# Hybrid encoder block on one core: steps that take another engine's result put off in a queue between matmuls

## The chip, the cores and the metric

The kernel runs on one core of a Trainium2 chip. Its engines work side by side, each through its own list of instructions in order: TensorE (PE, matmuls and transposes), VectorE (DVE), ScalarE (ACT), GpSimd (POOL), and SyncE (SP), which here only issues DMA transfers. An instruction starts when those ahead of it on its engine are through and what it reads or overwrites is free. The metric is the device time of one execution in microseconds (us); less is better.

## The reference

One block of a bidirectional encoder, in float32, on 1024 tokens of width 1024 (`D_MODEL`), with one input projection, gated linear attention with 4 heads, a pooling branch with 4 channel groups, a merge, and a feed-forward part (SwiGLU, inner width 2816):

```python
h = rmsnorm(x, norm_mix[l])
proj = h @ w_in[l]
q, k, v, r, lr_f, lr_b, u, g_a, g_b = jnp.split(proj, split_points, axis=-1)
...
o = o_fwd + o_bwd
o = o * lax.rsqrt(jnp.mean(o * o, axis=-1, keepdims=True) + EPS)
...
o = (o * jax.nn.silu(r.astype(jnp.float32))).astype(x.dtype)
y_a = o @ w_branch_gla[l]

pooled = multiscale_pool(u)
y_b = jnp.einsum('blgc,gcd->blgd', pooled, w_pool_group[l]).reshape(bsz, length, D_MODEL)
y_b = (y_b * pool_scale[l]).astype(x.dtype)

merged = jax.nn.sigmoid(g_a) * y_a + jax.nn.sigmoid(g_b) * y_b
x = x + merged @ w_out[l]

h2 = rmsnorm(x, norm_ffn[l])
gate, up = jnp.split(h2 @ w_ffn_in[l], 2, axis=-1)
x = x + (jax.nn.silu(gate) * up) @ w_ffn_out[l]
...
return rmsnorm(x, norm_final)
```

`o_fwd` and `o_bwd` are the scans of the attention in both directions, in chunks; `multiscale_pool` takes centred means over 2, 4, 8 and 16 tokens, less the token.

## The kernel before

**Products.** Each float32 operand is split in two: a high part, the cast to the matmul type (`wh`, `dh`, `oh`, `ph`: a cast on ACT, line 182), and a low part, the operand less its high part (`wl`, `dl`, `ol`, `pl`: a subtract on VectorE or POOL, line 183). A product is three matmuls, high by high, high by low and low by high, of 128x128 by 128x512 (line 256). The helper `split_to` writes the cast and, right behind it, the subtract. Large projections take seven products of half size in place of eight (Strassen's scheme as Winograd arranged it): sums of blocks are made ahead of products, sums of results behind them.

**Stages**, in order of time: the norm of `x`; the projections of queries, keys and values with the attention beside them (25 to about 345 us); the output gate and its transposes (to 393); ten gate runs of seven products, for pool input and merge gates (393 to 606), with the pooled sums beside them; the branch projection with `w_branch_gla` (606 to 690), whose results are merged with the gates; the projection with `w_out` (to 776); the units of the feed-forward part (to about 1200); its output projection (to 1415); the end.

**Order.** The program is written out by one Python function, and each engine executes in the order in which the function came to its instructions. Work for the other engines is spread between the matmuls by `pump(dt)`, called after each product of three, with 1 for 512 columns (three matmuls, 0.68 us) and 0.5 for 256. It moves three lists on: `pending` (weights to be split), `aside` (jobs that `beside` writes one step at a time, `every` so many units) and `side` (generators: the attention, `pooling` and `features`, each `yield` being the units until its next step).

**Names that the change touches.**
- `branch_piece` makes what a product of the branch projection needs: `load` issues the DMA of the weights (`wraw`), `sums` the block sums of the attention's output (`ob`, `t`, on VectorE), `make` the two casts and subtracts of the weights (`wh` on ACT, `wl` on POOL) and then `data_split`, the cast `dh` and subtract `dl`. `merged_piece` does the same in the `w_out` projection, from the merged blocks `mg` and their sums `s`, with the data first. `project` calls `line_make` one piece ahead.
- `merge` and `collect_branch` take the results of the branch off TensorE's banks: three operations per bank (lines 1326, 1328, 1329).
- `Gates.run` takes the results of a gate run off the banks: sums `ga` on VectorE (line 1194), a copy (1189) or sigmoid (1197) on ACT.
- `pooled` makes the pooled sums of a group (`ws`, VectorE) and splits them (`ph`, `pl`); `pooling` loads their input `u`, and stores the parts in `p_out`. `load_pool_weights` and `split_pool_weights` bring the group's small weights (`wpr`, split in `wph` and `wpl`), `load_pooled` the parts back.
- The raw weights of the gate runs are `fraw`, their block sums `fs`.
- `features` transposes the normed rows `xn` and splits them for the feed-forward units.
- `whole(t)` is the final norm and the store of a block of 128 rows: squares on ACT, `n3rs` on VectorE and POOL, the scaling `res` on VectorE, and the store on SP. It is called for four blocks, where the fifth of the seven products of the last projection ends. `split_piece` splits the next operands there (`wor`, `gor` to `oh`, `ol`).

Of the kernel before, what the change touches and what calls it, by code (L numbers as in the profile page):

```python
# [17 lines left out]
P = 128  # L18
# [25 lines left out]
PUT = 3  # L44
POOLING = 2.2

# [5 lines left out]
def kernel(  # L52
# [93 lines left out]
    pending, credit = [], [0.0]  # L146

    def pump(dt):
        if pending:
            credit[0] += dt  # L150
            if credit[0] >= 2:
                credit[0] = 0.0
                pending.pop(0)()
        if aside:
            aside[0][1] -= dt
            if aside[0][1] <= 0:
                cost = next(aside[0][0], None)
# [354 lines left out]
    def unit_jobs(n):  # L512
# [5 lines left out]
        for op, p, src in (  # L518
            (None, 1, a11), (None, 4, a22), (None, 2, a12), (partial(padd, a22, a21, a22), 5, a22),
            (partial(psub, a21, a11, a21), 7, a21), (partial(psub, a11, a22, a11), 6, a11),  # L520
            (partial(psub, a12, a12, a11), 3, a12),
        ):
            yield op, src, u_out[n][p]
# [32 lines left out]

    def beside(jobs, every, put):

        cast = differ = None
        puts = [[] for _ in range(put)]  # L560
        while True:
            job = next(jobs, None)
            if not any((job, cast, differ, *puts)):
                return
# [3 lines left out]
            if differ:  # L568
# [4 lines left out]
                else:  # L573
                    right.setdefault(dst, []).append((hi, lo))
            differ = None
            if cast:
# [3 lines left out]
                differ = src, parts, dst  # L580
            cast = None
            if job:
                op, src, dst = job
                if op:
                    op()
                if src is not None:
                    cast = src, dst
# [5 lines left out]
    def prepare_beside(jobs, every, put=PUT):  # L593
        aside.append([beside(chain(*jobs), every, put), every])

# [19 lines left out]
    def attention(h, q, k):  # L615
# [120 lines left out]
        kts = {(1, 1): transposed_keys(1, 1)}  # L736
        yield 5.0
        while h not in v_heads:
# [25 lines left out]
        p = scores(0)  # L764
        yield 4.5
        o = [slot(shape=(4, DV), s="o") for _ in range(2)]
# [209 lines left out]
    def pooled(g, u, hi, lo):  # L976
        width = WINDOWS[g]
        n = HALF + 2 * PAD
        for half in range(2):
# [18 lines left out]
            yield 1  # L998
            split_to(hi[:, half, :], lo[:, half, :], s[:, body])
            yield 1  # L1000


# [34 lines left out]
    def data_split(src):  # L1037
        hi, lo = slot(F32R, s="dh"), slot(F32R, s="dl")
        split_to(hi[:, :, :], lo[:, :, :], src[:, :, :])
        return [(hi[:, k, :], lo[:, k, :]) for k in range(2)]  # L1040
# [27 lines left out]
    def branch_piece(p, c):  # L1068
# [10 lines left out]
        def make(raw):  # L1079
            b = {1: ob[0, 0], 2: ob[1, 0], 3: ob[1, 1], 4: ob[1, 0], 5: ob[0, 0], 6: t2s, 7: ob[0, 1]}[p][c]  # L1080
            return weight_split(raw), data_split(b)

# [60 lines left out]
    def pooling():  # L1143

        for g in range(GROUPS):
# [7 lines left out]
            for cost in pooled(g, u, hi, lo):  # L1153
                yield POOLING * cost
            yield 2
            for n, t in enumerate((hi, lo)):
# [72 lines left out]
    for n, run in enumerate(gate_runs):  # L1229
# [4 lines left out]
        if n == 7:  # L1234
            finish_side()
            finish_beside()
            prepare_beside(map(unit_jobs, range(READY)), 3.2, 1)
        if last:
            finish_beside()
        for at, (of, p) in enumerate(run):  # L1240
# [7 lines left out]
            if at == 4:  # L1248
                flush()
                if n == 2:  # L1250
                    begin(pooling(), 4)
            if n >= 6:
                if at == 0:
                    load_pool_weights(n - 6)
                if at == (0 if last else 3):
                    load_pooled(n - 6)
                elif at == 4:
                    split_pool_weights(n - 6)
            if last and at == 1:
# [15 lines left out]
    def project(base, products, collect, before, amid=None, first=FIRST, up=UP, pools_of=lambda p: U_BANKS if p == 1 else X_BANKS):  # L1275
        banks = {}
        for at, p in enumerate(products):
# [4 lines left out]
            for c in range(2):  # L1282
                n = base + 2 * at + c
                while len(made) <= n:
                    line_make()
                line_load()
                line_make()
# [342 lines left out]

    begin(features(1), 10)
    zs = {n: Gated(units[n], True) for n in range(3)}
# [49 lines left out]
    def whole(t):  # L1682

        ms, res = vec(4, "n3ms"), slot(shape=(D,), s="res")
        for j in range(2):
            squares(t, ms, res, j)
        rs = two_scale(ms)
        for j in range(2):
            nc.vector.scalar_tensor_tensor(
                res[:, COLS[j]], x2[t][:, COLS[j]], rs[:, :], gain_final[:, COLS[j]], op0=ALU.mult, op1=ALU.mult  # L1690
            )
        nc.sync.dma_start(out[t * P : (t + 1) * P, :], res[:, :])

# [43 lines left out]
    for at, p in enumerate(OUT_ORDER):  # L1737
# [4 lines left out]
        for i in range(CLOSE if closing else n_of):  # L1742
# [6 lines left out]
            for m in range(4):  # L1749
# [9 lines left out]
        if closing:  # L1759
            for m in range(4):  # L1760
                for i in range(CLOSE, n_of):
# [31 lines left out]
```

## Time and profile before

| | |
|---|---|
| median of 3 runs | 1425.53 us (1422.4 to 1426.63) |
| profiled execution | 1426.57 us |
| span of the profile | 1424.9 us |
| TensorE busy | 1379.3 us, 97% |
| VectorE, ACT, POOL busy | 857.6, 623.0, 746.2 us |
| mean granted TensorE clock | 0.992 |
| DMA | 243.62 MB, 171 GB/s over the span |

The span goes from the first to the last record of the profile, and the 1.7 us between it and the execution's time lie around it. TensorE is the engine that is busy nearly all the time, so its waits, and the stretches in which its granted clock is below 1, are what the profile has to be searched for. Each row of the waits names an engine and what it waited for last; the timelines give the start of each instruction, its duration, and in brackets the engine's idle time ahead of it.

### The profile page before, as it was taken

The numbers are of one execution on the slowest core, as the hardware profiler recorded it, in microseconds if no ns is written. First come the engines' busy times: TensorE is split into PE (matmuls) and PEld (weight loads), VectorE is DVE, ScalarE is ACT, GpSimd is POOL, SyncE is SP. The second block draws the span as 40 slices with busy tenths as digits, with TensorE's granted clock in tenths as the row PEclk, the third lists the DMA queues.
The fourth block names the chain that finished last, engine by engine and source line by source line (L and its number), as shares of the span: only waits on it lengthen the run. The fifth ranks groups of instructions, "written<-read, shape, count | busy, mean of one in ns | idle before, by whom it ended". The sixth has DMA issues, their size and how long they took to land. (4 is left out here: it accounts for less than half of the span.)

```text
span 1424.9 us, 18551 instructions
## 1 busy us (share of the span) xinstructions
PE 1379.3 (97%) x6677; PEld 1157.4 (81%) x6677; DVE 857.6 (60%) x1073; ACT 623.0 (44%) x1115; POOL 746.2 (52%) x558
## 2 busy tenths in 40 slices
PE   7999999999999999899999999999999999999997
PEld 6889898978888788677877788888888888888876
DVE  6166757667645674677875775565655556343374
ACT  6364655553234344453346633333333334443253
POOL 3252715123298455464665176666666667564254
PEclk9999999999999999999999999999999999999999
DMA  6221422322277568896513565544444447975361
GB/s 189 75 60 45 139 69 98 126 94 70 75 238 236 177 217 278 333 386 202 194 60 142 177 228 170 169 150 148 143 149 151 144 158 257 389 258 190 133 266 59
DMA packets 167612, 243.62 MB, mean 171 GB/s; under 512 B 10936, under 2 KB 98016, under 8 KB 167520
## 3 DMA queue, kind: packets, MB, share of 16 engines
q1 hardware_dynamic: 167520, 242.45, 50.4%
q8 instruction: 52, 0.85, 0.3%
q14 instruction: 40, 0.33, 0.1%
HBM read 164.55 MB, written 77.86 MB: 170 GB/s over the span
## 5 line engine op out<-in xcount | busy, mean ns | idle before, releaser
L183 POOL TENSOR_TENSOR wl<-fs,wh 128x512 fp32r<-128x512 f32 x120 | 166.2, 1389 | 174.7 <-ACT wh L182 130.9
L256 PE MATMUL ps<-gh,wh 128*128 128x512 f32 x616 | 240.4, 390 | 0.0
L256 PE MATMUL ps<-gl,wh 128*128 128x512 f32 x616 | 239.8, 389 | 0.0
L256 PE MATMUL ps<-gh,wl 128*128 128x512 f32 x616 | 239.7, 389 | 0.0
L183 POOL TENSOR_TENSOR wl<-fraw,wh 128x512 fp32r<-128x512 f32 x90 | 129.4, 1438 | 57.3 <-ACT wh L182 57.2
L256 PE MATMUL ps<-hh,wh 128*128 128x512 f32 x376 | 149.9, 399 | 0.0
L256 PE MATMUL ps<-hh,wl 128*128 128x512 f32 x376 | 146.8, 390 | 0.0
L256 PE MATMUL ps<-hl,wh 128*128 128x512 f32 x376 | 146.5, 390 | 0.0
L183 POOL TENSOR_TENSOR wl<-raw,wh 128x512 fp32r<-128x512 f32 x47 | 67.3, 1444 | 145.6 <-ACT wh L182 120.8
L183 POOL TENSOR_TENSOR ol<-gor,oh 128x1024 fp32r<-128x1024 f32 (+1 forms) x42 | 103.5, 2472 | 74.0 <-ACT oh L182 67.2
L256 PEld LDWEIGHTS ps<-gl,wh 128*128 128x128 f32 x616 | 115.6, 188 | 24.2 <-DVE gl L1395 0.4
L256 PEld LDWEIGHTS ps<-gh,wl 128*128 128x128 f32 x616 | 115.6, 188 | 24.0
L256 PEld LDWEIGHTS ps<-gh,wh 128*128 128x128 f32 x616 | 115.7, 188 | 23.6
L256 PE MATMUL ps<-ol,oh 128*128 128x512 f32 x308 | 120.6, 392 | 3.0 <-DVE ol L183 3.0
L256 PE MATMUL ps<-oh,oh 128*128 128x512 f32 x308 | 120.6, 392 | 1.4 <-DVE x L1716 1.4
L256 PE MATMUL ps<-oh,ol 128*128 128x512 f32 x308 | 120.3, 391 | 0.0
L183 POOL TENSOR_TENSOR wl<-wraw,wh 128x512 fp32r<-128x512 f32 x56 | 86.7, 1574 | 54.6 <-ACT wh L182 46.3
L183 DVE TENSOR_TENSOR ol<-wor,oh 128x1024 fp32r<-128x1024 f32 (+1 forms) x42 | 72.3, 1742 | 48.0 <-ACT oh L182 40.6
L182 ACT CAST wh<-fs 128x512 fp32r<-128x512 f32 x120 | 73.7, 615 | 32.5 <-DVE fs L852 28.8
L256 PEld LDWEIGHTS ps<-hh,wl 128*128 128x128 f32 x376 | 70.6, 188 | 15.2
L256 PEld LDWEIGHTS ps<-hl,wh 128*128 128x128 f32 x376 | 70.7, 188 | 13.2
L256 PEld LDWEIGHTS ps<-hh,wh 128*128 128x128 f32 x376 | 70.7, 188 | 13.3
(249 smaller groups left out, 3188.5 us busy)
## 6 DMA issues: line engine op xcount, KB each, us to landing
fraw<-in_w_ffn_in_dram SPq DMA_DIRECT2D x44, 512.0 KB, 6.0
gor<-g_out SPq DMA_DIRECT2D x35, 512.0 KB, 6.2
raw<-in_w_in_dram SPq DMA_DIRECT2D x48, 256.0 KB, 3.0
g_out<-s SPq DMA_DIRECT2D x44, 256.0 KB, 2.3
fraw<-in_w_in_dram SPq DMA_DIRECT2D x20, 512.0 KB, 6.6
wor<-t_out SPq DMA_DIRECT2D x20, 512.0 KB
g_out<-g SPq DMA_DIRECT2D x33, 256.0 KB, 2.6
x<-in_x_dram SPq DMA_DIRECT2D x16, 512.0 KB, 5.7
```

The lines of the kernel that those rows point to most:

```text
L182: nc.scalar.copy(hi, src)
L183: eng.tensor_tensor(lo, src, as_f32(hi), op=ALU.subtract)
L256: nc.tensor.matmul(ps, a[i], b[j], start=first and n == 0, stop=last and n == 2, skip_group_check=onto)
```

## The change

A fourth list, `put_off`, holds steps for later: `soon(delay, *steps)` puts them in, `pump` writes those whose delay has run out, `settle` writes all. In it go the low parts `dl` of the data in the branch and `w_out` projections (2 units after the cast), the scale of `whole` (2 units after the squares) and the rest of `whole` with its store (1.5 after that). In `branch_piece` the data is cast ahead of the weights. The queue is settled ahead of each piece that `project` takes up, and at the closing products.

```diff
+    put_off = []
+
+    def soon(delay, *steps):
+        put_off.extend([delay, step] for step in steps)
+
+    def settle():
+        while put_off:
+            put_off.pop(0)[1]()
+
     def pump(dt):
+        for entry in put_off:
+            entry[0] -= dt
+        while put_off and put_off[0][0] <= 0:
+            put_off.pop(0)[1]()
         if pending:
...
     def data_split(src):
-        hi, lo = slot(F32R, s="dh"), slot(F32R, s="dl")
-        split_to(hi[:, :, :], lo[:, :, :], src[:, :, :])
+        hi, lo = (slot(F32R, s=s)[:, :, :] for s in ("dh", "dl"))
+        src = src[:, :, :]
+        nc.scalar.copy(hi, src)
+        soon(2, partial(nc.vector.tensor_tensor, lo, src, as_f32(hi), op=ALU.subtract))
         return [(hi[:, k, :], lo[:, k, :]) for k in range(2)]
...
-            return weight_split(raw), data_split(b)
+            right = data_split(b)
+            return weight_split(raw), right
...
                 n = base + 2 * at + c
+                settle()
                 while len(made) <= n:
                     line_make()
+                    settle()
...
             squares(t, ms, res, j)
-        rs = two_scale(ms)
-        for j in range(2):
...
+        def scale():
+            rs = two_scale(ms)
+            soon(1.5, partial(finish, rs))
+
+        def finish(rs):
+            for j in range(2):
...
+            nc.sync.dma_start(out[t * P : (t + 1) * P, :], res[:, :])
+
+        soon(2, scale)
```

The pooled sums are spread otherwise: their steps come every 1.75 units in place of 2.2, cast and subtract of the split are two steps, and the stores come 4 units after in place of 2. The group's weights are loaded and split earlier in the gate runs. `beside` can hold its casts back by `lag` steps, which the jobs at run 7 use (`lag` 2), and the order of the first two blocks that these jobs prepare is turned. In the attention two delays are longer, and the features begin later.

```diff
-POOLING = 2.2
+POOLING = 1.75
...
             yield 1
-            split_to(hi[:, half, :], lo[:, half, :], s[:, body])
+            nc.scalar.copy(hi[:, half, :], s[:, body])
             yield 1
+            nc.vector.tensor_tensor(lo[:, half, :], s[:, body], as_f32(hi[:, half, :]), op=ALU.subtract)
+            yield 0.2
...
-            yield 2
+            yield 4
             for n, t in enumerate((hi, lo)):
                 nc.sync.dma_start(p_out[g][n], as_f32(t[:, :, :]))
...
-            prepare_beside(map(unit_jobs, range(READY)), 3.2, 1)
+            prepare_beside(map(unit_jobs, range(READY)), 3.1, 1, 2)
...
-            if n >= 6:
-                if at == 0:
-                    load_pool_weights(n - 6)
-                if at == (0 if last else 3):
-                    load_pooled(n - 6)
-                elif at == 4:
-                    split_pool_weights(n - 6)
+            if 5 <= n < 9 and at == 5:
+                load_pool_weights(n - 5)
+            elif n >= 6 and at == 2:
+                split_pool_weights(n - 6)
+            if n >= 6 and at == (0 if last else 3):
+                load_pooled(n - 6)
...
-        yield 5.0
+        yield 5.6
...
-        yield 4.5
+        yield 5.2
...
-            begin(features(0), 10)
+            begin(features(0), 11.5)
...
-    begin(features(1), 10)
+    begin(features(1), 12)
```

**Where it moves instructions.** First, the branch projection on VectorE, from the third product's sums to the first operation of `merge` (the names end in buffer numbers; `t_...` is the sum `t`). Before:

```order
L183 TENSOR_TENSOR dl_6032<-ob_5805,dh_6031 128x1024
L1062 TENSOR_TENSOR ob_5796<-ob_5833,ob_5796 128x1024
L1064 TENSOR_TENSOR t_1184_6036<-ob_5837,ob_5796 128x1024
L183 TENSOR_TENSOR dl_6081<-t_1184_6036,dh_6080 128x1024
L1062 TENSOR_TENSOR ob_5797<-ob_5834,ob_5797 128x1024
L1064 TENSOR_TENSOR t_1196_6085<-ob_5838,ob_5797 128x1024
L183 TENSOR_TENSOR dl_6122<-t_1196_6085,dh_6121 128x1024
L1326 TENSOR_TENSOR ps_6066<-ps_6066,sum_5967 128x512
```

And now, at the same place:

```order
L1080 TENSOR_TENSOR ob_5796<-ob_5837,ob_5796 128x1024
L1082 TENSOR_TENSOR t_1184_6035<-ob_5841,ob_5796 128x1024
L162 TENSOR_TENSOR dl_6024<-ob_5805,dh_6023 128x1024
L1080 TENSOR_TENSOR ob_5797<-ob_5838,ob_5797 128x1024
L1082 TENSOR_TENSOR t_1196_6084<-ob_5842,ob_5797 128x1024
L162 TENSOR_TENSOR dl_6073<-t_1184_6035,dh_6072 128x1024
L162 TENSOR_TENSOR dl_6114<-t_1196_6084,dh_6113 128x1024
L1346 TENSOR_TENSOR ps_6066<-ps_6066,sum_5967 128x512
```

Each pair of sums stands ahead of the `dl` that it stood behind, and the two last `dl` are together right ahead of the merge.

On ACT, a little earlier, at the first two pieces of the branch, before:

```order
L182 CAST wh_5880<-wraw_5800 128x512
L182 CAST wh_5884<-wraw_5800 128x512
L182 CAST dh_5888<-ob_5796 128x1024
L1197 ACTIVATE ga_5794<-ga_5794 128x512
L1197 ACTIVATE ga_5767<-ga_5767 128x512
```

And now:

```order
L1056 CAST dh_5880<-ob_5796 128x1024
L196 CAST wh_5883<-wraw_5800 128x512
L196 CAST wh_5887<-wraw_5800 128x512
L1216 ACTIVATE ga_5794<-ga_5794 128x512
L1216 ACTIVATE ga_5769<-ga_5769 128x512
```

The data's cast changed places with the two of the weights.

Second, the four final norms on VectorE, from the first sum `x` of the product behind which they come to the next `ol`. Before:

```order
L1716 TENSOR_TENSOR x_2134_10852<-ps_11493,x_2134_10852 128x512
L1461 TENSOR_SCALAR n3rs_11897<-n3ms_11893 128x1
L1689 SCALAR_TENSOR_TENSOR res_11894<-x_2134_10852,n3rs_11897,gfin_10843 128x512 x2
L1716 TENSOR_TENSOR x_2141_10890<-ps_11494,x_2141_10890 128x512
L1461 TENSOR_SCALAR n3rs_11911<-n3ms_11907 128x1
L1689 SCALAR_TENSOR_TENSOR res_11908<-x_2141_10890,n3rs_11911,gfin_10843 128x512 x2
L183 TENSOR_TENSOR ol_11918<-wor_11850,oh_11917 128x1024
L1716 TENSOR_TENSOR x_2148_10928<-ps_11495,x_2148_10928 128x512
```

And now:

```order
L1743 TENSOR_TENSOR x_2134_10852<-ps_11493,x_2134_10852 128x512
L1743 TENSOR_TENSOR x_2141_10890<-ps_11494,x_2141_10890 128x512
L197 TENSOR_TENSOR ol_11906<-wor_11850,oh_11905 128x1024
L1481 TENSOR_SCALAR n3rs_11916<-n3ms_11893 128x1
L1743 TENSOR_TENSOR x_2148_10928<-ps_11495,x_2148_10928 128x512
L1481 TENSOR_SCALAR n3rs_11927<-n3ms_11901 128x1
L1743 TENSOR_TENSOR x_2155_10966<-ps_11496,x_2155_10966 128x512
L1714 SCALAR_TENSOR_TENSOR res_11894<-x_2134_10852,n3rs_11916,gfin_10843 128x512 x2
L1481 TENSOR_SCALAR n3rs_11945<-n3ms_11920 128x1
```

The scaling `res` of a block stands behind the sums of all four, and the first `ol` ahead of all four.

Third, the gate runs on SP, around the second and third store of pooled parts. Before:

```order
L1157 DMA p_out<-ph_4745 128x1024
L1157 DMA p_out<-pl_4746 128x1024
L844 DMA fraw_4855<-in_w_in_dram 128x8x128
L1149 DMA u_4864<-u_rows_4147 128x520
L1150 DMA u_4865<-u_rows_4147 128x520
L450 DMA sa_out<-ga_4635 256x1x512
L450 DMA sa_out<-ga_4659 256x1x512
L844 DMA fraw_5001<-in_w_in_dram 128x8x128
L844 DMA fraw_5024<-in_w_in_dram 128x8x128
L1157 DMA p_out<-ph_4890 128x1024
```

And now:

```order
L1176 DMA p_out<-ph_4745 128x1024
L1176 DMA p_out<-pl_4746 128x1024
L1168 DMA u_4854<-u_rows_4147 128x520
L1169 DMA u_4855<-u_rows_4147 128x520
L858 DMA fraw_4861<-in_w_in_dram 128x8x128
L464 DMA sa_out<-ga_4636 256x1x512
L464 DMA sa_out<-ga_4661 256x1x512
L858 DMA fraw_5003<-in_w_in_dram 128x8x128
L1176 DMA p_out<-ph_4879 128x1024
```

The weights' load `fraw` that stood between the stores and the loads of `u` stands behind the loads of `u`, and the next run's second one behind the stores as well.

More of the change, by code (lines that the diff above doesn't have):

```diff
@@ L518, in unit_jobs @@
         for op, p, src in (
-            (None, 1, a11), (None, 4, a22), (None, 2, a12), (partial(padd, a22, a21, a22), 5, a22),
+            (None, 4, a22), (None, 1, a11), (None, 2, a12), (partial(padd, a22, a21, a22), 5, a22),
             (partial(psub, a21, a11, a21), 7, a21), (partial(psub, a11, a22, a11), 6, a11),
@@ L555, in parts_for, with beside @@
         return [slot(F32R, s=s)[:, :, :] for s in ("trh", "trl")]
-    def beside(jobs, every, put):
-        cast = differ = None
+    def beside(jobs, every, put, lag):
+        casts, differ = [None] * lag, None
         puts = [[] for _ in range(put)]
@@ L562, in beside @@
             job = next(jobs, None)
-            if not any((job, cast, differ, *puts)):
+            if not any((job, *casts, differ, *puts)):
                 return
@@ L574, in beside @@
                     right.setdefault(dst, []).append((hi, lo))
-            differ = None
+            differ, cast = None, casts.pop(0)
             if cast:
@@ L580, in beside @@
                 differ = src, parts, dst
-            cast = None
+            casts.append(None)
             if job:
@@ L586, in beside @@
                 if src is not None:
-                    cast = src, dst
+                    casts[-1] = src, dst
                 elif dst is not None:
@@ L591, in beside, with prepare_beside @@
             yield every
-    def prepare_beside(jobs, every, put=PUT):
-        aside.append([beside(chain(*jobs), every, put), every])
+    def prepare_beside(jobs, every, put=PUT, lag=1):
+        aside.append([beside(chain(*jobs), every, put, lag), every])
     def finish_beside():
@@ L1686, in whole @@
             squares(t, ms, res, j)
-        rs = two_scale(ms)
-        for j in range(2):
[L1689 to L1692, printed above, removed]
+        def scale():
[3 more added lines that the diff above has]
+            for j in range(2):
+                nc.vector.scalar_tensor_tensor(
+                    res[:, COLS[j]], x2[t][:, COLS[j]], rs[:, :], gain_final[:, COLS[j]], op0=ALU.mult, op1=ALU.mult
+                )
+            nc.sync.dma_start(out[t * P : (t + 1) * P, :], res[:, :])
+        soon(2, scale)
     def second_half(t):
@@ L1759 @@
         if closing:
+            settle()
             for m in range(4):
```

## The prediction

> **What bounds the kernel now.** I read the page's first part, then the waits of TensorE, then windows of its time, and last the timelines of the engines behind each wait. The first fence has the row of the page on TensorE and the rows of the waits view that matter here (engine, line, what was waited for: us in total, times, longest).
>
> ```profile
> PE 1379.3 (97%) x6677; PEld 1157.4 (81%) x6677; DVE 857.6 (60%) x1073; ACT 623.0 (44%) x1115; POOL 746.2 (52%) x558
> PE ps L256 <- DVE ga L1194: 5.3, 2, 2.9
> PE ps L256 <- DVE dl L183: 4.3, 1, 4.3
> PE tr L1410 <- DVE xn L292: 3.7, 3, 2.2
> PE ps L256 <- POOL wl L183: 3.5, 7, 1.3
> PE ps L256 <- DVE ol L183: 3.0, 1, 3.0
> PE ps L256 <- ACT ga L1189: 1.4, 2, 1.0
> PE yb L256 <- ACT wph L182: 1.2, 1, 1.2
> ```
>
> TensorE is busy 1379.3 of the 1424.9 us of the span, so 45.6 us are all that waiting costs directly, some 10 of them the tail behind the last matmul. The change takes no matmul away: it can only win back waits and what hangs on them. The windows show that (start:end, length, TensorE busy, its matmuls, granted clock, DMA share, GB/s).
>
> ```profile
> 475.00:500.00 25.00, 21.81 (x89) 0.93 0.54 168
> 495.21:498.62 3.41, 3.41 (x10) 0.50 0.01 2
> 600.00:625.00 25.00, 22.82 (x100) 1.00 1.01 382
> 641.98:648.81 6.83, 5.05 (x12) 0.50 0.70 224
> ...
> 720.51:723.92 3.41, 3.41 (x9) 0.50 0.00 0
> 800.00:825.00 25.00, 25.00 (x111) 1.00 0.43 146
> 1372.43:1375.85 3.42, 3.42 (x10) 0.50 1.03 408
> ```
>
> At 800–825 nothing is waited for: 111 matmuls. In 475–500 there are 89, because a wait of 2.9 us is followed by 3.41 us in which the clock is 0.50. Such a stretch costs half of its busy time, 3.41/2 = **1.7 us**; the one at 642–649 costs 5.05/2 = **2.5 us**. Two more of 3.41 us lie behind the waits at 718 (for POOL) and 1368 (for VectorE). So a wait of about 3 us costs 4.6, if its clock stretch goes with it.
>
> [...]
>
> **Branch projection: the data cast ahead of the weights, the subtract put off.** Timelines: start, us, engine, line, operands, and in brackets idle time before it.
>
> ```profile
> 597.22 1.14 ACT L182 CAST wh<-wraw 128x512 fp32r<-128x512 f32 x2 [3.28 <-DMA wraw<-in_w_branch_gla_dram]
> 598.26 1.05 ACT L182 CAST dh<-ob 128x1024 fp32r<-128x1024 f32 x1
> ...
> 622.15 1.14 ACT L182 CAST wh<-wraw 128x512 fp32r<-128x512 f32 x2 [4.03 <-DMA wraw<-s_out]
> 623.20 1.05 ACT L182 CAST dh<-t 128x1024 fp32r<-128x1024 f32 x1
> ```
> ```profile
> 599.35 2.17 DVE L183 TENSOR_TENSOR dl<-ob,dh 128x1024 fp32r<-128x1024 f32 x1 [4.95 <-ACT dh L182]
> 601.44 0.68 DVE L1194 TENSOR_TENSOR ga<-ps,ga 128x512 f32<-128x512 f32 x1
> ...
> 624.27 2.21 DVE L183 TENSOR_TENSOR dl<-t,dh 128x1024 fp32r<-128x1024 f32 x1 [5.97 <-ACT dh L182]
> 626.41 2.31 DVE L1062 TENSOR_TENSOR ob<-ob,ob 128x1024 f32<-128x1024 f32 x1
> ...
> 633.20 0.69 DVE L1326 TENSOR_TENSOR ps<-ps,sum 128x512 f32<-128x512 f32 x1
> ...
> 641.47 4.45 DVE L183 TENSOR_TENSOR dl<-ob,dh 128x1024 fp32r<-128x1024 f32 x2
> ```
> ```profile
> 622.85 7.01 POOL L183 TENSOR_TENSOR wl<-wraw,wh 128x512 fp32r<-128x512 f32 x4 [6.89 <-ACT wh L182]
> 628.21 0.39 PE L256 MATMUL ps<-dh,wh 128*128 128x512 f32 x1
> 643.76 0.80 PE L256 MATMUL ps<-dl,wh 128*128 128x512 f32 x1 [4.28 <-DVE dl L183]
> ```
>
> First place: ACT stands 3.28 us for weights from DRAM, then casts them, and only then the data `dh`, whose load was issued before that of the weights. VectorE stands 4.95 us for `dh`, and the gate sum `ga` that frees TensorE's bank is behind that `dl`. With `dh` first, `dl` no longer waits for the weights: at least 1.14 us (the two casts) and at most 1.14 + 3.28 earlier, and TensorE's wait there was 2.4 (the 5.3 of the row for `ga` less the 2.9 at 491). I take the whole: **−2.4** (bounds −1.1 and −2.4).
>
> Second place: the same at 622, with 5.97 us of idle VectorE, and behind that `dl` stand the sums of the next column (`ob` 2.31 us, then `t`), its `dl`, and the twelve merge operations that start at 633.20. TensorE wants the `dl` of 641.47 at 639.1 and gets it at 643.8. After, the sums stand ahead of the `dl`, so they fill the 5.97 idle us; the `dh` cast no longer waits for `wraw`. The last thing ahead of the merges is then the second column's `dl`, whose `dh` on ACT still stands behind two weight casts of 622.15: 622.15 + 1.14 + 1.05 + 2.2 for the `dl` = 626.5. The merges come 633.2 − 626.5 = 6.7 us earlier, against 4.3 needed: **−4.3 and −2.5** of clock, −6.8. Bounds: 0, if the product still waits for its weights, and −6.8.
>
> What is late next: TensorE comes up to 5 us earlier to this stage, but at 600–625 the DMA engines are busy all the time (1.01), so weights land no earlier. Those cast at 622.15 are through POOL at 622.85 + two of about 1.3 = 625.4, and TensorE wants them at 628.2: 2.8 us of slack against 5. I give **+2.2** back here and +0.5 for the same at 575–600, bounds 0 and +5.
>
> **w_out projection.** The fence shows the chain that ends in the wait for `wl` at 718.
>
> ```profile
> 707.91 1.74 DVE L183 TENSOR_TENSOR dl<-mg,dh 128x1024 fp32r<-128x1024 f32 x1
> 709.58 2.30 DVE L1106 TENSOR_TENSOR s<-mg,mg 128x1024 f32<-128x1024 f32 x1
> ...
> 711.96 2.39 POOL L1107 TENSOR_TENSOR mg<-mg,mg 128x1024 f32<-128x1024 f32 x1 [1.16 <-DVE s L1106]
> 717.29 3.05 POOL L183 TENSOR_TENSOR wl<-wraw,wh 128x512 fp32r<-128x512 f32 x2 [2.94 <-ACT wh L182]
> ```
>
> The sum `s` starts the chain, and stands behind a `dl` of 1.74 us. Put off, that `dl` goes behind it, and the chain comes 1.2 to 1.7 us earlier, against waits of 1.3 + 0.3. Most goes, and with it most likely the clock stretch: **−2.5** (bounds −1.2 and −3.3).
>
> **Closing: final norm and stores.**
>
> ```profile
> 1365.52 0.21 DVE L1461 TENSOR_SCALAR n3rs<-n3ms 128x1 f32<-128x1 f32 x1 [0.79 <-ACT res L1455]
> 1366.40 1.41 DVE L1689 SCALAR_TENSOR_TENSOR res<-x,n3rs,gfin 128x512 f32<-128x512 f32 x2 [0.66 <-POOL n3rs L1462]
> 1367.73 3.37 DVE L183 TENSOR_TENSOR ol<-wor,oh 128x1024 fp32r<-128x1024 f32 x1
> ```
> ```profile
> 1353.45 14.72 SPq L1692 DMA_DIRECT2D out_dram<-res  x4
> ```
>
> For each of the four row blocks VectorE stands 0.79 us for the squares and 0.66 for POOL's power, then does 1.41 us of scaling, and the `ol` of 1367.73 is behind all four. TensorE waits 3.0 for it. In the new order the same operations stand ahead of this `ol`, but the waits between (4 × 1.45 = 5.8 us) are filled with the sums and the scaling of other blocks; that is more than 3.0. SP too holds loads back: the four stores keep its queue from 1353.45 to 1368.2, and the next load of pieces stood behind them; now one load of `wor` and `gor` is ahead. **−3.0 and −1.7**, −4.7 (bounds −1.5, if one of the four waits is filled and the clock stretch stays, and −4.7).
>
> **Gate runs.** The waits at 491 hang on weights:
>
> ```profile
> 477.64 0.54 SPq L844 DMA_DIRECT2D fraw<-in_w_in_dram  x1
> 478.28 1.41 SPq L1149 DMA_DIRECT2D u<-u_rows  x1
> ...
> 483.75 0.69 DVE L852 TENSOR_TENSOR fs<-fraw 128x512 f32<-128x512 f32 x1 [5.90 <-DMA fraw<-in_w_in_dram]
> ```
>
> VectorE idles 5.90 us for a load that SP issues behind two stores of pooled rows. In the new order it falls behind two loads of `u` too, 1.41 us for the first and somewhat less for the second, so about 2 us later, and in the next two runs likewise, in one of them behind the stores as well. On the other side the pooled sums and the cast `ph` are spread out and come ahead of a gate activation, which frees VectorE of waiting behind them by as much. I take **−0.5**, between −3 (the wait gone) and +5 (a wait like the one at 491 once more). The pool weights are loaded and split earlier: the row for `wph` was 1.2, **−1.2** (bounds 0, −1.2). Casts two steps late and sums a little earlier touch the row of ACT's `ga`, 1.4: **−0.9** (0, −1.4). The features begin 1.5 and 2 pump units later, which shifts the transposes that wait for `xn` (3.7): TensorE has 1 to 1.4 us more of other work ahead of them, but the norm behind `xn` is no faster: **−0.7** (+0.7, −1.4).
>
> **Attention.** Its waits are 6 us in small pieces (rows below 1.4 each); key products come a small product later: **−0.5** (+1.5, −2). ACT gets two more table loads there:
>
> ```profile
> 286.05 1.28 ACT L953 ACT_TABLE_LOAD   x1
> ```
>
> Two of 1.28 are 2.6 us on an engine that is busy 44% of the span; the bounds take them in. [...]
>
> **Sum.** −2.4 − 6.8 − 2.5 − 4.7 − 0.5 − 1.2 − 0.9 − 0.7 − 0.5 = −20.2; with +2.7 given back −17.5. The profiled execution took 1426.57, 1.0 above the median of 1425.53: 1426.57 − 17.5 = **1409**.
>
> **The rivals.**
> *Half of it.* TensorE early only runs into the next limit: the saturated loads at 592–622, then POOL's `wl`, which are no faster. For it: slack of 2.8 against 5 us. Against: VectorE idles 5 and 6 us there, which is what goes. With half the gain lost in the branch and at the closing (5.7) and the give-back at its bound (+2.3): about 1417.
> *The change doesn't do what it says.* The put-off steps come back in the same place, since a put-off subtract is released by products that themselves wait. Then only the small terms (−2.4 to −3) are left: about 1424. Against: the instruction order does differ where the waits are.
> *Slower.* With data first, both weight casts and POOL's subtract queue behind data that comes late. The w_out stage works that way already, and its wait at 718 is of this kind: 1.6 plus 1.7 of clock, 3.3 each. The branch has 14 such casts; from the seventh column on that is late by over 2.8 us (the slack above), 7 × 3.3 = 23 outweigh the 17.5: 1409 + 23 = 1432. Against: sums ahead of `dl` make `dh` earlier, not later.
> *Nearly all.* Without give-back, and with what is left of the wait for `xn` (3.0) and of the one at 491 (2.9 + 1.7 − 0.5 = 4.1) gone too: 1409 − 2.7 − 7.1 = 1399.
>
> **How the numbers follow.** Forecast 0.56, half 0.21, no effect 0.08, slower 0.07, nearly all 0.08. About 0.3%, 4.3 us, is what can be told from no change. Forecast, half and nearly all are faster by more: 0.85; no effect is the same: 0.08; slower 0.07. The range goes from 1399 (nearly all) to 1420 (half, with three more us lost in the gate runs, within their bound); outside lie no effect, slower and a few per cent below.
>
> **What would show it.** The waits of TensorE for `dl` and `ol` gone and `ga` down to one row of about 3; granted clock 1.00 in 625–650 and 1350–1375, still below 1 in 475–500; VectorE without the 5.97 idle ahead of the branch sums; the `wl` row below 3.5. The forecast is wrong if a new wait of over 2 us stands in 600–690, or if the 491 wait has grown and come a second time near 515.

## The result, and the profile after

The changed kernel took **1407.44 us** in the median of six runs (1406.17 to 1408.86), the kernel before 1427.26 in six beside them (1422.4 to 1430.26). The ratio is 0.9862 with a 95% interval of 0.9843 to 0.9882: 1.4% faster. The profiled execution took 1407.11, with a span of 1405.4, against 1426.57 and 1424.9 before: 19.5 us less. The forecast was 1409 in a range of 1399 to 1420. One execution among all those below, of the run with the pooled sums as before, took 2242.18 us at a mean granted clock of 0.575 and is left out of that run's ratio.

First the row of the page on the engines, and the rows of TensorE's waits (us in total, times, longest).

```profile
PE 1371.3 (98%) x6677; PEld 1153.1 (82%) x6677; DVE 842.7 (60%) x1073; ACT 625.6 (45%) x1117; POOL 748.8 (53%) x558
```
```profile
PE ps L270 <- POOL wl L197: 3.3, 6, 1.0
PE ps L270 <- DVE ga L1213: 3.2, 2, 2.3
PE tr L1430 <- DVE xn L306: 1.6, 1, 1.6
PE ps L270 <- DVE x L1743: 1.4, 1, 1.4
PE ps L270 <- DVE dl L162: 0.7, 1, 0.7
PE ps L270 <- ACT ga L1208: 0.5, 1, 0.5
PE ps L270 <- DVE ol L197: 0.2, 1, 0.2
```

The 4.3 us for `dl` are 0.7, the 3.0 for `ol` 0.2, the 1.2 for `wph` have no row among these. The row for `ga` is 3.2 where 5.3 stood, and is not the same wait: the windows show where it lies now.

```profile
475.00:500.00 25.00, 23.16 (x100) 1.00 0.55 187
500.00:525.00 25.00, 21.61 (x86) 0.93 0.56 177
600.00:625.00 25.00, 25.00 (x112) 1.00 1.03 405
625.00:650.00 25.00, 25.00 (x112) 1.00 0.91 349
1350.00:1375.00 25.00, 23.37 (x102) 1.00 0.73 274
```

At 600 to 650 TensorE is at its full 112 matmuls per window and a clock of 1.00, though the DMA engines are as full as before (1.03). At 475–500 there are 100 matmuls in place of 89, but at 500–525 only 86: in the gate runs a new wait has come, with a slow stretch of its own.

Both programs have the same 6677 matmuls, so the two traces can be laid side by side by their count. The table has the time of the changed kernel's trace against that of the kernel before at the same matmul (minus: earlier), and what each stage gave of it, beside the term of the forecast.

| up to (us of before) | against before, us | of this stage | forecast |
|---|---|---|---|
| 334, attention | −2.2 | −2.2 | −0.5 |
| 539, about the first seven gate runs | +1.1 | +3.2 | −0.5 |
| 587, the later gate runs | −1.3 | −2.3 | −2.1 (`wph`, ACT's `ga`) |
| 614, last gate run | −3.9 | −2.6 | −2.4 |
| 689, branch projection | −11.3 | −7.4 | −6.8, +2.7 given back |
| 738, `w_out` to its middle | −14.3 | −3.0 | −2.5 |
| 805, transposes | −15.2 | −0.8 | −0.7 |
| 1376, to the last projection | −19.4 | −4.3 | −4.7 |

How the branch looks now, on ACT and on VectorE (start, us, engine, line, operands, idle time before it):

```profile
614.12 1.05 ACT L1056 CAST dh<-t 128x1024 fp32r<-128x1024 f32 x1
619.93 1.14 ACT L196 CAST wh<-wraw 128x512 fp32r<-128x512 f32 x2 [4.76 <-DMA wraw<-s_out]
620.98 1.05 ACT L1056 CAST dh<-t 128x1024 fp32r<-128x1024 f32 x1
```
```profile
614.62 1.23 DVE L1082 TENSOR_TENSOR t<-ob,ob 128x1024 f32<-128x1024 f32 x1
615.76 1.22 DVE L162 TENSOR_TENSOR dl<-t,dh 128x1024 fp32r<-128x1024 f32 x1
622.06 2.20 DVE L162 TENSOR_TENSOR dl<-t,dh 128x1024 fp32r<-128x1024 f32 x1 [5.08 <-ACT dh L1056]
624.18 0.68 DVE L1346 TENSOR_TENSOR ps<-ps,sum 128x512 f32<-128x512 f32 x1
```

ACT stands longer than before for its weights (4.76 us against 4.03), and VectorE nearly as long for the `dh` behind them (5.08 against 5.97). The waits are still there; but the sums and the first `dl` are done by then, and the merges start at 624.18 in place of 633.20, of which 3.9 us are the lead with which the stage begins. TensorE waits for nothing there.

### The profile page after: what moved, and what is told of

It is laid out like the page before. It is cut to its first block, busy times and chain, and to the rows that moved or that the text cites. A ratio compares the mean times of both kernels' runs of the same rounds, so it can differ in the third digit from the quotient of the medians.

```text
span 1405.4 us, 18561 instructions
## 1 busy us (share of the span) xinstructions
PE 1371.3 (98%) x6677; PEld 1153.1 (82%) x6677; DVE 842.7 (60%) x1073; ACT 625.6 (45%) x1117; POOL 748.8 (53%) x558
## 4 chain that ended last, share of the span: by engine, by line
PE 74%; DVE 8%; issue 5%; POOL 5%; ACT 4%; DMA 3%; SPq 0%; POOLq 0%; DVEq 0%; ACTq 0%
PE ps L270 67%; POOL wl L197 2%; DMA fraw<-in_w_in_dram 2%; PE op L797 2%; PE kv L270 1%; PE sc L733 1%; PE op L270 1%; DVE fs L866 1%; PE tr L317 1%; DVE z L666 1%; PE ps L448 1%; POOL fraw L599 1%; DVE res L1714 1%; ACT wh L196 0%; DMA wor<-t_out 0%
## 5 line engine op out<-in xcount | busy, mean ns | idle before, releaser
L197 POOL TENSOR_TENSOR ol<-gor,oh 128x1024 fp32r<-128x1024 f32 (+1 forms) x42 | 100.2, 2392 | 93.3 <-ACT oh L196 84.8
L270 PEld LDWEIGHTS ps<-gl,wh 128*128 128x128 f32 x616 | 115.7, 188 | 25.1 <-DVE gl L1415 1.3
L270 PEld LDWEIGHTS ps<-gh,wl 128*128 128x128 f32 x616 | 115.7, 188 | 24.0
L270 PEld LDWEIGHTS ps<-gh,wh 128*128 128x128 f32 x616 | 115.7, 188 | 23.6
L197 DVE TENSOR_TENSOR ol<-wor,oh 128x1024 fp32r<-128x1024 f32 (+1 forms) x42 | 62.0, 1496 | 54.0 <-ACT oh L196 46.7
```

The costliest lines, as they stand in the source:

```text
L197: eng.tensor_tensor(lo, src, as_f32(hi), op=ALU.subtract)
L270: nc.tensor.matmul(ps, a[i], b[j], start=first and n == 0, stop=last and n == 2, skip_group_check=onto)
```

## The experiments

Each was timed in three rounds, unless said otherwise, together with the kernel before on the same chip, and its ratio is to that kernel. The experiments ran on four chips, so between them the ratios and traces count beside the medians. Where a trace is said to lose or win, it is against the first trace of the changed kernel, at the same matmul. "Undone" means as in the kernel before.

**The weights cast first again** (the low parts stay put off):

```diff
-            right = data_split(b)
-            return weight_split(raw), right
+            return weight_split(raw), data_split(b)
```

> The changed kernel with one line undone: in the branch projection the weights are cast ahead of the data again; the low parts stay put off. If the order of the casts carries the gain in the branch stage, the wait for `ga` at the end of the gate runs comes back (+2.4 us) and the first merge comes at about 628.7 in the clock of before, so that the wait for `dl` comes back in part (0 to 3 us, with up to 2.5 of clock): 1410 to 1415. If the put-off subtract carries it (the sums ahead of `dl`), only the 2.4 come back or nothing: 1407 to 1410, and no wait for `dl` at 630 to 640.

Measured: 1409.66 us, ratio 0.9888 (0.9874 to 0.9903). The wait for `ga` at 598.6 came back, 1.95 us, and the trace lost 2.3 us there. At 639 nothing came back:

```profile
622.53 4.44 DVE L162 TENSOR_TENSOR dl<-t,dh 128x1024 fp32r<-128x1024 f32 x2 [3.64 <-ACT dh L1056]
626.89 0.69 DVE L1345 TENSOR_TENSOR ps<-ps,sum 128x512 f32<-128x512 f32 x1
```

VectorE still waits for a `dh` behind weights, but with both sums done it then has only the two `dl` ahead of the merges. For the first place the order of the casts is the cause; for the second it isn't needed.

**The low parts at once** (the data stays ahead of the weights):

```diff
-        soon(2, partial(nc.vector.tensor_tensor, lo, src, as_f32(hi), op=ALU.subtract))
+        nc.vector.tensor_tensor(lo, src, as_f32(hi), op=ALU.subtract)
```

> The changed kernel with the low part `dl` subtracted at once in the branch and w_out projections, the data still cast ahead of the weights. If the order of the casts carries the branch, nothing comes back there, and the wait for POOL's `wl` comes back in the w_out projection (2.8 us of shift between the traces there): 1410 to 1411. If the put-off carries the branch, the 4.3 us wait for `dl` and its slow clock come back too: 1416 to 1418.

Measured: 1410.28 us, ratio 0.9891 (0.9876 to 0.9906). Nothing came back in the branch, so the put-off isn't needed there either, as long as the data is cast first. And in the `w_out` projection the wait for `wl` came back with 0.75 + 0.29 us only, where the changed kernel waits 0.71 us for `dl`, and no slow stretch: 0.6 us lost. The larger part of the loss stood behind it, at 746: a wait of 2.3 us for VectorE's `x` (1.2 in the changed kernel) with a slow stretch, of which the wait for `xn`, gone here, gave some back. The trace is that of the fastest of the four executions, 1407.44 us; the others took 1410.16 to 1410.93, at a lower mean clock (0.995 to 0.996 against 0.998). So not all that the median lost can be read from it.

**Both undone:** the two diffs above together.

> The changed kernel with both steps of the branch undone: weights cast ahead of the data, and `dl` subtracted at once; all else kept. One of the two alone was enough to keep the wait for `dl` at 639 away. If they are two ways to the same thing, both undone bring it back: the wait of 4.3 us with up to 2.5 us of slow clock, beside the 2.2 us at 600 that the order of the casts alone brought: 1414 to 1418. If the wait went because the stage now begins at another phase (the gate runs, the loads), it stays away: 1409 to 1411.

Measured: **1419.42 us**, ratio 0.9942 (0.9927 to 0.9957): 12 us over the changed kernel, and more than expected. The waits view and VectorE at that place:

```profile
PE ps L270 <- DVE ga L1212: 5.2, 3, 2.3
PE ps L270 <- POOL wl L197: 4.8, 8, 1.3
PE ps L270 <- DVE dl L1057: 4.2, 1, 4.2
```
```profile
623.29 2.20 DVE L1057 TENSOR_TENSOR dl<-t,dh 128x1024 fp32r<-128x1024 f32 x1 [5.84 <-ACT dh L1056]
625.41 2.31 DVE L1080 TENSOR_TENSOR ob<-ob,ob 128x1024 f32<-128x1024 f32 x1
...
632.21 0.69 DVE L1345 TENSOR_TENSOR ps<-ps,sum 128x512 f32<-128x512 f32 x1
```

It is the picture of before: 5.84 us of idle time ahead of a `dl`, the sums behind it, the merges at 632. Either step alone takes this wait away, neither is needed beside the other. Between this run and the one before it, all engines but ACT have the same instructions in the same order, and ACT differs in where its casts of the branch stand: 1419.4 against 1410.3, 9 us (7 by the ratios, since the two ran on different chips) for the order of casts on an engine that is busy 45% of the time in the changed kernel. The wait for POOL's `wl` in `w_out` came back too, with 1.27 + 0.28 us and its slow stretch, 2.8 us in all. The order of the `w_out` stage is the same in the two runs, and in the one the wait is 1.04 us and the stage loses 0.6, in the other it is 1.55 with a slow stretch, and the stage loses 2.8: the larger part comes only together with what the branch left over.

**The final norms at once:**

```diff
-            soon(1.5, partial(finish, rs))
+            finish(rs)
...
-        soon(2, scale)
+        scale()
```

> The changed kernel with the four final norms written at once, as before, and all else kept. If they were what made `ol` late, the wait at the last projection comes back with its slow clock stretch: +4.3 us, the shift between the two traces there, so 1411.7, and all before it is unchanged. If the wait went because everything before came at another phase, 1407 to 1408.

Measured: 1411.09 us, ratio 0.9901 (0.9887 to 0.9916). The wait is back, with a slow stretch behind it, and the trace is half a us early up to there and 3.8 us late at 1357, so 4.2 us lost (3.4 at 1381, as the next wait is shorter). The row of the waits, and the window:

```profile
PE ps L270 <- DVE ol L197: 3.0, 1, 3.0
```
```profile
1350.00:1375.00 25.00, 21.51 (x87) 0.93 0.86 326
```

But that `ol` begins late behind the norms is the smaller part of it. The first fence is of this run, the second of the changed kernel, where this `ol` still stands behind eight scaling operations (the last two are shown):

```profile
1351.85 2.57 POOL L197 TENSOR_TENSOR ol<-gor,oh 128x1024 fp32r<-128x1024 f32 x1 [1.09 <-ACT oh L196]
1352.13 3.38 DVE L197 TENSOR_TENSOR ol<-wor,oh 128x1024 fp32r<-128x1024 f32 x1
```
```profile
1346.21 5.33 POOL L197 TENSOR_TENSOR ol<-gor,oh 128x1024 fp32r<-128x1024 f32 x2
1346.42 5.68 DVE L1714 SCALAR_TENSOR_TENSOR res<-x,n3rs,gfin 128x512 f32<-128x512 f32 x2
1352.03 2.35 DVE L197 TENSOR_TENSOR ol<-wor,oh 128x1024 fp32r<-128x1024 f32 x2
```

TensorE runs dry at 1352.59 in this run and at 1353.05 in the changed kernel, and `ol` begins 0.5 us ahead of that here and 1.0 there: that is half a us of the 2.7 between the two waits. The other 2.2 us are its duration, 3.38 us here, beside POOL's subtract of `gor`, and 1.21 there, where POOL is through. There POOL's two subtracts lie beside the last two scalings instead, which take 2.88 us each where the six ahead of them take 0.74 or 0.75. The kernel before is like this run: 3.37 us from 1367.73, beside POOL's 2.57 us from 1367.45. POOL can begin earlier in the changed kernel because the cast of `gor` on ACT that it waits for is done at 1345.88 and not at 1351.77, where ACT stands behind squares that wait for VectorE's `x`. So putting the norms off does win these 4 us, but by what VectorE's and POOL's subtracts run beside.

**The loads of the gate runs one product earlier** than in the changed kernel, so that both stand ahead of the stores of the pooled parts:

```diff
-            if at in (1, 2) and not last:
+            if at in (0, 1) and not last:
                 gunits[n + 1].load()
```

> The changed kernel with the weights of the next gate run loaded one product earlier, so that both loads stand ahead of the stores of the pooled parts in SP's queue; nothing else. If the late load is what makes the waits of TensorE at 487 to 491 (1.8 us) and 508 to 515 (3.4 us and a slow clock stretch of 1.7), they go: 1401 to 1403. If VectorE's own queue of pooled sums and gate sums makes them, they stay: 1406.5 to 1408.

Measured: **1402.06 us**, ratio 0.984 (0.9824 to 0.9857). Of the waits between 480 and 520 one of 1.1 us is left, and the lead over the changed kernel is 5.6 us at the end. The two programs differ in the order on SP alone. What the change had made of the loads, in its own trace on SP and VectorE:

```profile
478.19 0.60 SPq L858 DMA_DIRECT2D fraw<-in_w_in_dram  x1
495.12 0.34 SPq L1176 DMA_DIRECT2D p_out<-ph  x1
496.18 0.34 SPq L1176 DMA_DIRECT2D p_out<-pl  x1
...
498.16 0.42 SPq L858 DMA_DIRECT2D fraw<-in_w_in_dram  x1
```
```profile
504.60 0.69 DVE L866 TENSOR_TENSOR fs<-fraw 128x512 f32<-128x512 f32 x1 [3.21 <-DMA fraw<-in_w_in_dram]
...
513.95 0.68 DVE L1213 TENSOR_TENSOR ga<-ps,ga 128x512 f32<-128x512 f32 x1
```

From 478.8 to 495.1 SP issues nothing: the store at its head waits 16.2 us for `ph`. The weights behind the stores and the loads of `u` land when VectorE has waited 3.2 us for them. From there on VectorE works without a wait, and the sum `ga` that TensorE waits for until 514.7 is behind a dozen of its instructions.

The same kernel again, in five rounds:

> The kernel with the loads one product earlier once more, in more rounds, since its interval and that of the changed kernel touched. If the 5.4 to 5.6 us by which its trace came earlier behind the gate runs hold, 1401 to 1403 and a ratio of 0.980 to 0.985. If they were the chance of slow clock stretches, 1404 to 1407.

Measured: **1400.07 us**, ratio 0.9811 (0.9789 to 0.9833), below the interval of the changed kernel. It is the fastest of all that ran, and beats both. Its trace, of the slowest of the five executions (1402.97), has the two windows of the gate runs so:

```profile
475.00:500.00 25.00, 25.00 (x112) 1.00 0.64 211
500.00:525.00 25.00, 23.99 (x105) 1.00 0.59 184
```

**The pooled sums as before:**

```diff
-POOLING = 1.75
+POOLING = 2.2
...
-            nc.scalar.copy(hi[:, half, :], s[:, body])
+            split_to(hi[:, half, :], lo[:, half, :], s[:, body])
             yield 1
-            nc.vector.tensor_tensor(lo[:, half, :], s[:, body], as_f32(hi[:, half, :]), op=ALU.subtract)
-            yield 0.2
...
-            yield 4
+            yield 2
```

> The changed kernel with the steps of the pooled sums as before (2.2 units in place of 1.75, cast and subtract in one step, stores 2 units after), which puts the loads of `fraw` back where they stood among the stores and the loads of `u`; all else kept. If the new spreading is what cost 3.2 us of shift between 334 and 540, it comes back as a gain: one wait of about 3 us at 490, none at 512, 1403 to 1406. If it did some good that the later load hides, there are two waits again: 1407 to 1410.

Measured: 1407.69 us, ratio 0.9856 (0.984 to 0.9873), which the median can't tell from the changed kernel, and which lies in the range of the second theory. The trace speaks for the first: it has one wait at 491.6, 2.87 us long and with a slow stretch as before the change, and none at 512, and by 540 it has first lost 2.2 us in the norm at the start, most of it to a slow stretch there, and then won 3.5. So in the gate runs the new spreading costs 3.2 to 3.5 us, by one trace of each.

**The pooled sums as before, with the early loads:** the two diffs above together.

> The changed kernel with the pooled sums' steps as before, and the gate runs' weights loaded one product earlier as in the run that moved only the loads (1402.1). If only the place of the load matters, it gives the same, 1401 to 1403. If the new spreading of the pooled sums is worth something once the load is out of the way (VectorE's gate sums stand behind `pl`, which waits for ACT), it is slower by the 1 to 3 us of such a wait: 1403 to 1405.

Measured: 1403.15 us, ratio 0.9825 (0.981 to 0.9839). Against 1402.06 and 1400.07 with the new spreading the intervals overlap; by the traces, the lead at the end is 1.9 us smaller than in the first of these and 0.5 than in the second. Waits of 0.95, 0.58 and 0.45 us stand where the new spreading has one of about 1.1. It may be worth something once the loads are out of the way; that isn't settled.

**The delays in the attention as before:**

```diff
-        yield 5.6
+        yield 5.0
...
-        yield 5.2
+        yield 4.5
```

> The changed kernel with the two delays in the attention as before (5.0 and 4.5), which takes the two added table loads of ACT away too. If the longer delays won the 2.2 us of shift up to 334, it comes back: 1409 to 1410. If the table loads cost TensorE something there, it is faster: 1405 to 1407.

Measured: 1410.34 us, ratio 0.9877 (0.9861 to 0.9894). Its trace loses 1.6 us to a slow stretch at the start, and then 2.1 us up to 334, with the waits of before at 115.7 (1.06 us), 232.4 (1.26) and 304.2 (1.42). So the delays win the 2.1 us, although they bring ACT two table loads more. Which of the two delays it is was not tried.

**The pooled branch's weights, and the jobs beside run 7 on, as before:**

```diff
-            (None, 4, a22), (None, 1, a11), (None, 2, a12), (partial(padd, a22, a21, a22), 5, a22),
+            (None, 1, a11), (None, 4, a22), (None, 2, a12), (partial(padd, a22, a21, a22), 5, a22),
...
-            prepare_beside(map(unit_jobs, range(READY)), 3.1, 1, 2)
+            prepare_beside(map(unit_jobs, range(READY)), 3.2, 1)
...
-            if 5 <= n < 9 and at == 5:
-                load_pool_weights(n - 5)
-            elif n >= 6 and at == 2:
-                split_pool_weights(n - 6)
-            if n >= 6 and at == (0 if last else 3):
-                load_pooled(n - 6)
+            if n >= 6:
+                if at == 0:
+                    load_pool_weights(n - 6)
+                if at == (0 if last else 3):
+                    load_pooled(n - 6)
+                elif at == 4:
+                    split_pool_weights(n - 6)
```

> The changed kernel with two parts as before: the pooled branch's weights loaded and split in the last gate runs (steps 0 and 4), and the jobs beside run 7 on with casts one step later in place of two, every 3.2, in the old order. If these parts won the waits for `wph` (1.2 us) and for ACT's `ga` (1.4, of which 0.5 is left), they come back: +1.2 + 0.9, 1409 to 1410. If those waits went because the runs before come at another time, 1407 to 1408.

Measured: 1410.01 us, ratio 0.9882 (0.9862 to 0.9901). The waits came back as expected: 1.1 us for `wph`, and 1.6 for ACT's `ga` where 0.5 was left; between 517 and 590 the trace loses 2.1 us. Which of the two parts brings which wait was not tried apart.

```profile
PE ps L270 <- ACT ga L1208: 1.6, 2, 1.2
PE yb L270 <- ACT wph L196: 1.1, 1, 1.1
```

**The features as before:**

```diff
-            begin(features(0), 11.5)
+            begin(features(0), 10)
...
-    begin(features(1), 12)
+    begin(features(1), 10)
```

> The changed kernel with both beginnings of the features as before (10 in place of 11.5 and 12). If the later beginnings only let TensorE do 1 to 1.4 us of other work ahead of transposes that wait for `xn`, the waits grow by as much, once or twice: +0.8 (the shift between the traces there) to +2.1, 1408 to 1409.5, and TensorE has two or three waits for `xn`. If the norm behind `xn` sets the time alone and the work is only moved, it is the same, 1407 to 1408.

Measured: 1407.79 us, ratio 0.987 (0.9848 to 0.9892): no difference that can be told. The waits for `xn` are 3.4 us in two in place of 1.6 in one, but 1.2 for `x` and 0.9 for `gl` have gone, and a slow stretch at 772 is in the profiled execution. By its trace 0.9 us are lost; this term stays open.

**The changed kernel again:**

> The changed kernel itself, beside the two others on one chip. Both theories expect 1406 to 1409. Its profile shows what chance does to the stretches of slow clock: none of the two theories says whether the wait of 2.3 us at 512 is followed by one again.

Measured: 1407.33 us, ratio 0.9859 (0.9838 to 0.988). Its profile has the same waits, and the slow stretch at 515 again.

## Why the prediction came out, point by point

- **Right, by mechanism and size:** the wait for `ga` behind a `dl` that waits for weights (−2.4; −2.6, and undoing the order of the casts alone brought 2.3 back), the pool weights and ACT's `ga` (−2.1; −2.3, and 2.1 came back).
- **Right in size, by luck, with the mechanism mostly wrong:** `ol` at the closing (−4.7; −4.3, and 4.2 came back when the norms were undone, 3.4 of it for good). The forecast filled 5.8 us of waits ahead of `ol` and let it begin that much earlier. Against the place where TensorE wants it, it begins only half a us earlier than before; two of the scalings ahead of it grew to 2.88 us each. The rest of the wait went because the subtract takes 1.21 us in place of 3.37, with POOL's subtract no longer beside it, and the forecast had no term for that.
- **Right in size, the reason only half:** the wait for `dl` in the branch. The forecast had two reasons, `dh` ahead of the weights and the sums ahead of `dl`, and added them to one picture. Each alone is enough, which only the run with both undone could show: no trace of one of them alone would have led there.
- **Right in size, the reason good for the smaller part only:** `w_out`, −2.5 against −3.0. The forecast put it on `dl` ahead of the sum `s`. With `dl` back there the stage lost 0.6 us in one run (waits of 1.04 us) and 2.8 in the other (1.55 us and a slow stretch), with the same order in that stage; most of the gain is that of the branch before it, and the slow stretch that is gone with it.
- **The step that failed most: "+2.7 given back".** The forecast took the landing of the weights as fixed, since the DMA engines were full, and held 2.8 us of slack against a lead of 5. The lead at that place was 3.9, and the weights were not fixed: SP issued the loads of the stage's next weights from 609.40 on in place of 614.26, and ACT cast them at 619.93 in place of 622.15, so 2.2 us earlier, with the DMA engines as full as before (1.03 in 600–625, 1.01 before). 1.7 us of slack were needed and 2.8 were there. The same 1.7 us are missing at the merges: forecast for 626.5 by the clock of before, 6.7 us earlier, they start at 624.18 + 3.9 = 628.1, 5.1 us earlier. That the 4.3 us of the wait went all the same was closer than the forecast thought.
- **The gate runs: "I take −0.5" was +3.2.** Its mechanism stood in the forecast as the upper bound (a wait like the one at 491 once more, +5), with the load of `fraw` behind the stores and the loads of `u`. The value was taken from the wrong side: that VectorE would be freed by as much. The run with the early loads showed which queue counts: SP's.
- **The attention: "−0.5, between +1.5 and −2" was −2.2**, just outside. The waits of 6 us in pieces were seen, but the term wasn't worked out from the pieces. The two added table loads of ACT, 1.28 us each, are in that −2.2, and the run with the delays undone, without them, gave back 2.1.
- **The three errors nearly cancel:** 2.7 not given back and 1.7 more in the attention, against 3.7 lost in the gate runs and small differences. So 1409 is closer to 1407.4 than the working deserves.
- **The rivals:** "half of it" and "nothing" didn't come. The slower one, weights queued behind late data in the branch, didn't either: TensorE has no wait there at all. Of the things that the profile was to show, the clock in 475–500 was expected below 1 and is 1.00; the loss stands in 500–525. Of the signs of being wrong one came by half: the wait at 491 shrank, from 2.87 us to 0.9, but a second one of 2.27 us came near 515.
- **A reading that was off and changed nothing:** behind the last matmul stand 6.8 of the 45.6 us, not some 10.

## What to carry to other kernels

A step that needs another engine's result should stand behind what the engine can do meanwhile: not to shorten its wait (it was 5.97 and is 5.08 us), but so that nothing that another engine needs stands behind it. When loads that others wait for share a queue with stores that wait for a result, issue the loads first: here that alone was worth 5 us and more, on top of the change. Compare how long steps take, not only when they start: at the closing a subtract of 1.21 us in place of 3.37 won more than its earlier start. And where two edits aim at the same wait, undo both together before saying which one did it.

## What the runs showed of the hardware beyond what was expected

**The length of a wait did not tell whether a slow stretch followed it.** The forecast counted a slow stretch with the waits at 639, 718 and 1368, and in the changed kernel's trace all three are gone with them. At 512 it is not so plain. The changed kernel waits 2.27 us there, and the run with the weights first nearly the same, 2.26 us (0.97 in the first of its windows and 1.29 in the second). Windows over the wait and the time behind it, first of the changed kernel, then of that run (window, length, TensorE busy, matmuls, granted clock, DMA share, GB/s):

```profile
512.16:515.57 3.41, 1.14 (x6) 1.00 0.01 2
515.57:518.99 3.42, 3.42 (x10) 0.50 0.00 0
```
```profile
511.05:514.46 3.41, 2.44 (x10) 1.00 0.01 2
514.46:517.87 3.41, 2.12 (x9) 1.00 0.01 2
517.87:521.29 3.42, 3.42 (x17) 1.00 0.00 0
```

In the first the clock is 0.50 for 3.42 us behind the wait, in the second it stays at 1.00: by the estimate of half a stretch's busy time, 1.7 us less for the same wait. In the kernel before, the wait of 2.38 us at 600 had no slow stretch behind it (1.00 in 600–625), and the shorter one of 1.28 + 0.29 us at 718 had one (0.50 in 720.51–723.92). What decides it, these runs do not show.

**A slow stretch also came where the programs do not differ.** In the profiled execution of the run with the attention's delays undone one lies in the norm of `x`, ahead of all that this run changes, and costs its trace 1.6 us. The first fence is of that run, the second of the changed kernel, whose clock is 1.00 there:

```profile
15.00:22.00 7.00, 5.07 (x27) 0.76 0.61 194
18.37:21.78 3.41, 3.19 (x15) 0.50 0.79 246
```
```profile
15.00:22.00 7.00, 5.16 (x41) 1.00 0.65 208
```

This is of the size by which executions of one kernel scatter here (1406.17 to 1408.86 in the six of the changed kernel), and why a term of 1 or 2 us is better read from traces laid side by side than from medians.

**Most subtracts of VectorE beside a tensor operation of POOL took longer, up to 3.42 us against 1.23.** VectorE's 128x1024 subtracts `dl` and `ol` took 1.21 to 1.23 us wherever no tensor operation of POOL ran beside them (15 times before, 23 in the changed kernel). Beside one they took 1.21 to 3.42 us before (32 of 48 over 1.23), and 1.21 to 2.85 now (22 of 40). In the pair shown above, POOL's began 0.28 us earlier, and VectorE's ended 1.09 us after POOL's had ended. What the two share, the runs do not show.
